# RWKV prepared two chunks at a time, with U of both heads in one PSUM bank and the rate kept as raw tanh

## The chip, the cores and the metric

The kernel runs on one core of one Trainium2 chip, in one launch. The metric is the device time of an execution in microseconds: 4006.45 before, the median of three runs (4003.45 to 4014.16).

## The reference

Two layers of a diffusion transformer with three token mixers side by side, all in fp32. 1024 latent tokens and 256 context tokens of width 1024 are normalised and projected; a gated linear attention, a grouped-query attention and an RWKV-7 branch of width 512 each give an output; three sigmoid gates weigh them, and a last projection is added to the residual. Only the RWKV branch is touched here. Cut to what matters, for 8 heads of 64, once forward and once backward over the tokens:

```python
w = jnp.exp(-RWKV_DECAY_SCALE * jax.nn.sigmoid(w0 + jnp.tanh(wd) @ wup))
a = jax.nn.sigmoid(a0 + ad @ aup)                 # the rate
kd = k * (1.0 + (a - 1.0) * k_a)                  # the key with its factor
def step(s, inp):                                 # token by token
    sa = jnp.einsum('bhvk,bhk->bhv', s, kk_t)
    s = (s * w_t[:, :, None, :] - sa[..., None] * (kk_t * a_t)[:, :, None, :]
         + v_t[..., None] * k_t[:, :, None, :])
    return s, jnp.einsum('bhvk,bhk->bhv', s, r_t)
```

The two directions are added, normalised per head, given a bonus term sum(r * (kf + kb) * r_k) * v and multiplied by silu of a gate.

## The kernel before

The scan is done in chunks of 64 tokens. Ten steps of 128 tokens, that is of two chunks c = 0, 1, go through each layer, and a step treats the forward block (d = 0) and the mirrored backward block (d = 1) together. Five pieces of code make up a step, each a Python generator whose `yield w` marks a place where other work may come between:

- **elem** (L863): loads lt, kk, k, r; eight program matmuls ps_t<-lt,wup per direction (the trace counts each fp32 matmul as two) give decay and rate before their tanh; ScalarE's tanh (L897) and GpSimd's `tensor_scalar` (L898) make the sigmoid (of the rate the negative one), VectorE's scan (L900) sums the decays, ScalarE's exponentials make Pt and its inverse, products on VectorE and GpSimd give AR (L910, L912) and BK (L920, L924). GpSimd multiplies kk by the rate (L919), forms the factor of the key in four quarters (L922), and multiplies by r for the bonus (L929), which goes out to wscr.
- **gram** (L933), for one chunk: eight program matmuls ps_t<-AR,BK for each direction, copied to Ms (ScalarE, L955) and under a mask to G (VectorE, L956); BK transposed to BKT. Ms goes to DRAM (nscr), and its 16x16 diagonal blocks come back as Lm. Thirty VectorE instructions on 64 partitions (mt L974 and acc L977 in turn) invert these unit triangles. The inverse goes out to tscr and, transposed, to dscr, and comes back whole as DT and Dg.
- **merge** (L990): the matmuls ps_u<-DT,G, then ps_u<-Dg,ET and two of ps_u<-T,ET build the inverse T of the whole 64x64 block.
- **chain** (L1027): the state. ps_a<-UV,G and ps_a<-S,AR make X, ps_a<-X,T makes U, which two copies (L1061 VectorE, L1063 ScalarE) write into UV; ps_a<-UV,BKT gives the next state S, and ps_a<-AR,S and ps_a<-G,UV the output.
- **finish** (L1119): normalisation and bonus of a block whose second direction is done.

`spread` interleaves generators by windows given as shares of a stage; `rwkv` (L1151) is a stage per chunk: the chain of chunk q over the whole of it, merge of q + 1, gram of q + 2, and in every other stage elem of the next step. `weave` puts this beside `merge_gates`, dense matmuls in triples of 512 columns (ps_mm or ps_o<-h,wh twice and <-h,wl once) that need nothing of RWKV and here are called fill; a fill matmul may be placed no earlier than eight yields before its place in the code. A scheduler then fixes the order of each engine's instructions, so that what stands in a queue waits for what is ahead of it. All DMAs are issued by SyncE's queue in the trace (SP), in order too, the fill's weights (wr) among them.

PSUM is used by tag: two banks "mm", two "a", two "t", one "u" and one "o".

Of the kernel before, what the change touches and what calls it, by code (L numbers as in the profile page):

```python
# [29 lines left out]
def consts():  # L30
# [8 lines left out]
    c["gmask"] = np.concatenate([np.concatenate([above, incl], 1), np.concatenate([strict, incl], 1)], 0)  # L39
# [26 lines left out]
    c["ident16"] = np.tile(np.eye(16, dtype=np.float32).reshape(1, 256), (64, 1))  # L66
# [4 lines left out]
def hybrid_kernel(ctx: ExitStack, tc: tile.TileContext, I: dict, C: dict, out: bass.AP):  # L71
# [102 lines left out]
    NSCR = 3  # L174
    nscr, dscr, tscr = [[dt(f"{x}scr{i}", [64, 1040]) for i in range(NSCR)] for x in "ndt"]

# [3 lines left out]
    def full(z):  # L180
        return z.rearrange("(u i) x -> u (i x)", i=4)[:, 0:4096].rearrange("u (s t) -> s u t", t=64)
# [120 lines left out]
    zero = zp.tile([64, 1040], F32, name="zero")  # L302
# [30 lines left out]
    for l in range(DEPTH):  # L333
# [73 lines left out]
        vec.tensor_scalar(out=prm[:, 6, :], in0=prm[:, 5, :], scalar1=-1.0, scalar2=None, op0=ALU.mult)  # L407
        vec.tensor_scalar(out=prm[:, 7, :], in0=prm[:, 5, :], scalar1=-1.0, scalar2=1.0, op0=ALU.mult, op1=ALU.add)
# [418 lines left out]
        gmask, id16 = rload("gmask", [128, 128]), rload("ident16", [64, 256])  # L827
# [35 lines left out]
        def elem(step):  # L863

            live = need_ctx or step >= 2
            o = {"AR": [], "BK": [], "PC": rp.tile([128, 2, 8], F32, tag="PC", bufs=3, name=nm("PC"))}
            ld = {}
            lt = re_.tile([128, 2, 128], F32, tag="lt", bufs=1, name=nm("lt"))
            for d in range(2):
                c = slice(128 * blk_of(step, d), 128 * blk_of(step, d) + 128)  # L870
                for j in range(2):
                    dma(out=lt[64 * j:64 * j + 64, d], in_=lora[64 * d:64 * d + 64, j, c])
                for x in ("kk", "k", "r"):
                    if x == "r" and not live:
                        continue
                    ld[x, d] = re_.tile([128, 4, 128], F32, tag="ld_" + x, bufs=2, name=nm("ld_" + x))
                    dma(out=ld[x, d], in_=rscr[x][:, c].rearrange("(m p) n -> p m n", p=128))
            for d in range(2):
                t0 = 128 * blk_of(step, d)

                def tk(x):
                    v = ld[x, d]
                    if d:
                        v = v[:, :, ::-1]
                    return v.rearrange("p m (c i) -> p m c i", c=2)

                sc, av = tmp(), tmp()
                pz = [ps("t"), ps("t")]
                for p in range(4):
                    for j in range(2):  # L890
                        hr = slice(64 * j, 64 * j + 64)
                        x = lt[hr, d, :]
                        pe.matmul(pz[j][:, 128 * p:128 * p + 128], wup[d][hr, 128 * p:128 * p + 128], x[:, ::-1] if d else x, start=True, stop=True)
                yield 1.8
                for j, dst, bi, s in ((0, sc, 0, 0.5), (1, av, 2, -0.5)):
                    for p in range(4):
                        act(out=dst[:, p, :], in_=pz[j][:, 128 * p:128 * p + 128], func=AF.Tanh, scale=0.5, bias=prm[:, bi + d, p:p + 1])  # L897
                    pool.tensor_scalar(out=dst, in0=dst, scalar1=s, scalar2=s, op0=ALU.mult, op1=ALU.add)  # L898
# [12 lines left out]
                if live:
                    vec.tensor_tensor(out=AR[:, :, :, 1, :], in0=Pv[:, :, :, 1:65], in1=tk("r"), op=ALU.mult)  # L912
                else:
                    vec.memset(AR[:, :, :, 1, :], 0.0)
                BK = rq.tile([128, 4, 2, 2, 64], F32, tag="BK", bufs=2, name=nm("BK"))
                av4 = av.rearrange("p m (c i) -> p m c i", c=2)
                ka = tmp()
                ka4 = ka.rearrange("p m (c i) -> p m c i", c=2)
                pool.tensor_tensor(out=ka4, in0=tk("kk"), in1=av4, op=ALU.mult)  # L919
                vec.tensor_tensor(out=BK[:, :, :, 0, :], in0=ka4, in1=Pi, op=ALU.mult)  # L920
                for p in range(4):
                    pool.tensor_scalar(out=av[:, p, :], in0=av[:, p, :], scalar1=prm[:, 6, p:p + 1], scalar2=prm[:, 7, p:p + 1], op0=ALU.mult, op1=ALU.add)  # L922
# [8 lines left out]
            return o

        def gram(q, es, step):  # L933

            c, e = q % 2, es[step]
            o = dict(e)
            G = rq.tile([128, 2, 2, 4, 128], F32, tag="G", bufs=3, name=nm("G"))
            BKT = rq.tile([128, 2, 4, 128], F32, tag="BKT", bufs=3, name=nm("BKT"))
            UV = rq.tile([128, 2, 4, 2, 64], F32, tag="UV", bufs=3, name=nm("UV"))
            Ms = rq.tile([64, 2, 2, 4, 64], F32, tag="Ms", bufs=1, name=nm("Ms"))  # L940
            o["G"], o["BKT"], o["UV"] = G, BKT, UV
            for d in range(2):
                t0 = 128 * blk_of(step, d)
                v = vtm[d, t0 + 64 * c:t0 + 64 * c + 64, :]
                dma(out=UV[64:128, d].rearrange("p m h i -> p (m h i)"), in_=v)
            for d in range(2):
                AR, BK = e["AR"][d], e["BK"][d]
                pg = [ps("t"), ps("t")]
                for p in range(4):
                    for h in range(2):  # L950
                        r = slice(64 * h, 64 * h + 64)
                        pe.matmul(pg[h][:, 128 * p:128 * p + 128], BK[r, p, c].rearrange("p a i -> p (a i)"), AR[r, p, c].rearrange("p a i -> p (a i)"), start=True, stop=True)
                yield 2.0
                for h in range(2):
                    act(out=Ms[:, h, d], in_=pg[h][0:64].rearrange("p (u i) -> p u i", u=4)[:, :, 0:64], func=AF.Copy)  # L955
                    vec.tensor_tensor(  # L956
                        out=G[:, h, d], in0=pg[h].rearrange("p (u i) -> p u i", u=4),
                        in1=gmask.unsqueeze(1).to_broadcast([128, 4, 128]), op=ALU.mult)
            ns, ds, ts = nscr[q % NSCR], dscr[q % NSCR], tscr[q % NSCR]
            dma(out=full(ns), in_=Ms.rearrange("p h d m t -> p (h d m) t"))  # L960
            Lm = rq.tile([64, 16, 16], F32, tag="Lm", bufs=1, name=nm("Lm"))
            dma(out=Lm, in_=diag(ns))
# [3 lines left out]
            for d in range(2):  # L966
                pt = ps("t")
                for p in range(4):
                    pe.transpose(pt[:, 128 * p:128 * p + 128], e["BK"][d][:, p, c].rearrange("p a i -> p (a i)"), ident)
# [401 lines left out]
```

## Time and profile before

| | |
|---|---|
| median of three runs | 4006.45 us (4003.45 to 4014.16) |
| the profiled execution | 3994.97 us, span 3993.2 us, mean granted clock 0.958 |
| TensorE busy | 3737.1 us, 94% |
| VectorE / ScalarE / GpSimd busy | 53% / 41% / 23% |
| the chain that ended last | TensorE 68%, DMA 11%, VectorE 8%, GpSimd 4% |
| DMA | 497 MB, mean 125 GB/s |

RWKV's first stretch lies at about 1040 to 1828 us (layer 0), the second at 3014 to 3752 us (layer 1). "Busy" is the time in which an instruction of the engine is under way; a matmul at the lower clock is busy for longer, so a high share is not yet full speed. Releasers in brackets say whose event ended a wait; where one instruction waited for several, the one that came last. A wait of an engine other than TensorE costs nothing as long as nobody on TensorE is reached by it.

### The profile page before, as it was taken

What the parts mean: (1) busy time and instruction counts of PE and PEld (TensorE: products, weight loads), DVE (VectorE), ACT (ScalarE), POOL (GpSimd) and SP (SyncE); (2) the same over time, 40 slices, a digit from 0 to 9 for tenths busy, and PEclk for the clock granted to TensorE, in tenths of its full rate; (3) what the DMA queues carried; (4) which work ended last, traced back from release to release, by engine and by line L of the source; (5) the groups of instructions that cost most, each with busy time, mean ns of one, the idle gap of its engine ahead of it and who ended that gap; (6) DMA issues with size and microseconds to landing.
All of it is one profiled execution on the core that took longest, in us unless ns stands there. A gap on an engine that the chain in (4) does not pass through costs nothing.

```text
span 3993.2 us, 82346 instructions
## 1 busy us (share of the span) xinstructions
PE 3737.1 (94%) x32356; PEld 3135.2 (79%) x32356; DVE 2101.7 (53%) x4932; ACT 1649.8 (41%) x4135; POOL 934.1 (23%) x1072
## 2 busy tenths in 40 slices
PE   5999999999889898899998999999998898988999
PEld 3699888888777787677877898888886776766787
DVE  3234445456576676654453244455565766665462
ACT  3244435456434444434133344354474334344322
POOL 2133220000232322310333042300002323223042
PEclk7999999999989999999999999999998899889999
DMA  7723225312365667556544132253124556655553
GB/s 228 247 59 89 55 79 169 103 54 84 99 146 124 143 157 187 146 135 193 159 139 132 52 96 70 76 159 116 48 70 108 117 128 143 152 136 134 178 157 113
DMA packets 826613, 497.24 MB, mean 125 GB/s; under 512 B 303152, under 2 KB 760176, under 8 KB 824176
## 3 DMA queue, kind: packets, MB, share of 16 engines
q1 hardware_dynamic: 826224, 491.97, 45.0%
q8 instruction: 254, 4.16, 0.5%
q14 instruction: 135, 1.11, 0.1%
HBM read 340.02 MB, written 151.81 MB: 123 GB/s over the span
## 4 chain that ended last, share of the span: by engine, by line
PE 68%; DMA 11%; DVE 8%; POOL 4%; issue 4%; ACT 3%; SPq 2%; POOLq 0%; DVEq 0%; ACTq 0%
PE ps_mm L85 27%; PE ps_a L85 17%; PE ps_o L85 12%; PE ps_u L85 6%; PE ps_t L90 3%; PE ps_t L85 2%; DMA nscr<-Ms 2%; DMA Lm<-nscr 2%; POOL tmp L922 1%; DVE mt L974 1%; DVE acc L977 1%; DMA wr<-in_w_in_dram 1%; DVE wl L343 1%; DMA tscr<-acc 1%; POOL tmp L919 1%
## 5 line engine op out<-in xcount | busy, mean ns | idle before, releaser
L85 PE MATMUL ps_mm<-h,wh 128*128 128x512 f32 (+1 forms) x2496 | 764.5, 389 | 10.1 <-ACT wh L342 7.7
L85 PEld LDWEIGHTS ps_mm<-h,wh 128*128 128x128 f32 x2496 | 452.5, 196 | 105.2 <-issue 11.7
L343 DVE TENSOR_TENSOR wl<-wr,wh 128x512 fp32r<-128x512 f32 (+1 forms) x464 | 334.5, 743 | 296.7 <-ACT wh L342 292.5
L85 PE MATMUL ps_mm<-h,wl 128*128 128x512 f32 (+1 forms) x1248 | 473.8, 380 | 1.7 <-DVE wl L343 1.7
L342 ACT ACTIVATE wh<-wr 128x512 fp32r<-128x512 f32 (+1 forms) x464 | 271.5, 622 | 420.1 <-PE ps_mm L85 161.4
L85 PE MATMUL ps_mm<-wh,h 128*128 128x256 f32 x2032 | 400.4, 290 | 9.5 <-ACT wh L342 5.9
L85 PEld LDWEIGHTS ps_mm<-wh,h 128*128 128x128 f32 x2032 | 327.7, 194 | 26.0 <-issue 10.7
L85 PE MATMUL ps_a<-h,wh 128*128 128x512 f32 (+1 forms) x1024 | 300.1, 369 | 0.0
L85 PE MATMUL ps_mm<-wl,h 128*128 128x256 f32 x1016 | 293.4, 289 | 0.4 <-DVE wl L343 0.2
L85 PE MATMUL ps_o<-h,wh 128*128 128x512 f32 (+1 forms) x928 | 287.7, 392 | 0.6 <-DVE M L1265 0.6
L85 PEld LDWEIGHTS ps_mm<-h,wl 128*128 128x128 f32 x1248 | 243.6, 195 | 47.8 <-issue 4.0
L974 DVE TENSOR_TENSOR mt<-Lm,acc 64x15 f32<-64x15 f32 (+2 forms) x600 | 129.4, 216 | 163.7 <-DMA Lm<-nscr 146.0
L803 POOL TENSOR_TENSOR y<-y,sg 128x128 f32<-128x128 f32 x64 | 30.2, 472 | 755.1 <-DVE nb L794 369.0
L85 PEld LDWEIGHTS ps_a<-h,wh 128*128 128x128 f32 x1024 | 183.7, 189 | 28.3
L85 PEld LDWEIGHTS ps_mm<-wl,h 128*128 128x128 f32 x1016 | 196.7, 194 | 7.4 <-issue 4.9
L85 PE MATMUL ps_o<-wh,h 128*128 128x256 f32 x976 | 196.7, 289 | 3.5 <-ACT h L286 3.2
L85 PEld LDWEIGHTS ps_o<-h,wh 128*128 128x128 f32 x928 | 167.9, 197 | 34.2 <-issue 2.2
L85 PE MATMUL ps_a<-h,wl 128*128 128x512 f32 (+1 forms) x512 | 188.6, 368 | 0.0
L776 DVE TENSOR_REDUCE mx<-ps_mm 128x1 f32<-128x512 f32 (+1 forms) x200 | 117.9, 594 | 111.1 <-PE ps_mm L85 108.0
L85 PE MATMUL ps_o<-h,wl 128*128 128x512 f32 (+1 forms) x464 | 176.1, 380 | 0.0
L85 PEld LDWEIGHTS ps_o<-wh,h 128*128 128x128 f32 x976 | 158.5, 193 | 10.7 <-issue 5.3
L1006 POOL COPY T<-Dg 128x512 f32<-128x512 f32 x40 | 30.0, 749 | 566.2 <-DMA Dg<-dscr 527.2
(326 smaller groups left out, 8125.2 us busy)
## 6 DMA issues: line engine op xcount, KB each, us to landing
wr<-in_w_in_dram SPq DMA_DIRECT2D x376, 256.0 KB, 3.5
tg<-th SPq DMA_DIRECT2D x96, 256.0 KB, 3.4
th<-tg SPq DMA_DIRECT2D x96, 256.0 KB, 2.9
wm<-in_w_mod_dram SPq DMA_DIRECT2D x16, 1024.0 KB, 7.1
ld_k<-rscr_k SPq DMA_DIRECT2D x40, 256.0 KB, 3.6
ld_kk<-rscr_kk SPq DMA_DIRECT2D x40, 256.0 KB, 3.7
UV<-vtm SPq DMA_DIRECT2D x80, 128.0 KB, 3.2
nscr<-Ms SPq DMA_DIRECT2D x40, 256.0 KB, 3.8
```

What stands on the lines that cost most here:

```text
L85: PE.last = nc.tensor.matmul(*a, **k)
L90: PE.last = nc.tensor.transpose(*a, **k)
L342: act(out=hi, in_=src, func=AF.Copy)
L343: vec.tensor_tensor(out=lo, in0=src, in1=hi.bitcast(F32), op=ALU.subtract)
L776: vec.tensor_reduce(out=mx[:, i:i + 1], in_=s[:, :n], axis=AX.X, op=ALU.max, negate=True)
L803: pool.tensor_tensor(out=y[:, hc], in0=y[:, hc], in1=sg[:, hc], op=ALU.mult)
L919: pool.tensor_tensor(out=ka4, in0=tk("kk"), in1=av4, op=ALU.mult)
L922: pool.tensor_scalar(out=av[:, p, :], in0=av[:, p, :], scalar1=prm[:, 6, p:p + 1], scalar2=prm[:, 7, p:p + 1], op0=ALU.mult, op1=ALU.add)
L974: vec.tensor_tensor(out=mt[:, :n, :w], in0=Lm[:, j, j + 1:16].unsqueeze(2).to_broadcast([64, n, w]), in1=acc[:, j:j + 1, :w].to_broadcast( ...
L977: vec.tensor_tensor(out=acc[:, j + 1:16, :w], in0=acc[:, j + 1:16, :w], in1=mt[:, :n, :w], op=ALU.add)
L1006: pool.tensor_copy(out=T.rearrange("p d m t -> p (d m t)"), in_=Dg.rearrange("p d m t -> p (d m t)"))
```

## The change

- `prep` takes the place of the windows for elem and gram: elem and gram of both chunks for d = 0, then for d = 1, then one `inverse` for both chunks on 128 partitions. Scratch tensors have 128 rows and there are two of each instead of three; DT takes a buffer of Ms (two in all), Dg has two, G and BKT have four; the UV load moves into merge.
- `rwkv` is a stage per step: both chains over the whole of it, merge of its second chunk in 0 to 0.35, prep of the next step in 0 to 0.6, merge of the next step's first chunk in 0.75 to 1.0.
- U of both heads goes into the two partition halves of one bank instead of two banks.
- The rate stays raw tanh: the scaling of it is left out, a VectorE instruction computes (tanh + 1) * kk where GpSimd multiplied, and the missing factor -0.5 stands in the mask of G, in the copies of Ms and (by `half`) of BKT. The factor of the key is made by four ScalarE copies with scale and bias instead of four GpSimd instructions.

The matmuls are the same in number and shape.

```diff
@@ key factor, rate
-                for j, dst, bi, s in ((0, sc, 0, 0.5), (1, av, 2, -0.5)):
...
-                    pool.tensor_scalar(out=dst, in0=dst, scalar1=s, scalar2=s, op0=ALU.mult, op1=ALU.add)
+            pool.tensor_scalar(out=sc, in0=sc, scalar1=0.5, scalar2=0.5, op0=ALU.mult, op1=ALU.add)
...
-                pool.tensor_tensor(out=ka4, in0=tk("kk"), in1=av4, op=ALU.mult)
+            vec.scalar_tensor_tensor(out=ka4, in0=av4, scalar=1.0, in1=tk("kk"), op0=ALU.add, op1=ALU.mult)
...
-                    pool.tensor_scalar(out=av[:, p, :], in0=av[:, p, :], scalar1=prm[:, 6, p:p + 1], scalar2=prm[:, 7, p:p + 1], op0=ALU.mult, op1=ALU.add)
+                act(out=BK[:, p, :, 1, :], in_=av4[:, p], func=AF.Identity, scale=prm[:, 6, p:p + 1], bias=prm[:, 7, p:p + 1])
@@ preparation
+        def prep(os, step):
+            e = {}
+            yield from elem(step, 0, e)
+            o = [chunk(step, c, e) for c in range(2)]
+            Ms = [None, None]
+            for c in range(2):
+                Ms[c] = rq.tile([64, 2, 2, 4, 64], F32, tag="Ms", bufs=2, name=nm("Ms"))
+                yield from gram(o[c], c, 0, Ms[c])
+            yield from elem(step, 1, e)
+            for c in range(2):
+                yield from gram(o[c], c, 1, Ms[c])
+                dma(out=full(nscr[step % NSCR], c), in_=Ms[c].rearrange("p h d m t -> p (h d m) t"))
+            yield from inverse(step, o)
+            os[2 * step], os[2 * step + 1] = o
...
-            Lm = rq.tile([64, 16, 16], F32, tag="Lm", bufs=1, name=nm("Lm"))
+            Lm = rq.tile([128, 16, 16], F32, tag="Lm", bufs=1, name=nm("Lm"))
...
+                if j % 5 == 4:
+                    yield 0.0
...
+            for c in range(2):
+                DT = o[c]["DT"] = rq.tile([64, 2, 2, 4, 64], F32, tag="Ms", bufs=2, name=nm("DT"))
+                dma(out=DT.rearrange("p h d m t -> p (h d m) t"), in_=full(ts, c))
@@ chain
-            pu = [ps("a"), ps("a")]
+            pu = ps("a")
...
-                        pe.matmul(pu[h][0:64, (4 * d + p) * 64:(4 * d + p) * 64 + 64], T[r, d, p, :], X[r, d, p, :], start=True, stop=True)
-            yield 1.8
+                        pe.matmul(pu[r, (4 * d + p) * 64:(4 * d + p) * 64 + 64], T[r, d, p, :], X[r, d, p, :], start=True, stop=True)
+            yield 1.3
@@ rwkv
-            for q in range(nq):
-                ths = [(chain(q, os.pop(q)), 0.0, 1.0, 8.3 + 6 * 2.0 + 12 * 2.0 if q % 2 else 8.3 + 6 * 2.0)]
-                if q + 1 < nq:
-                    ths.append((merge(os, q + 1), *((0.4, 0.9), (0.65, 1.0))[q % 2], 3.3 + 4 * 2.0))
-                if q + 2 < nq:
-                    ths.append((put(os, q + 2, gram(q + 2, es, (q + 2) // 2)), *((0.55, 0.9), (0.1, 0.5))[q % 2], 5.0 + 6 * 2.0))
...
+            for w in spread([(prep(os, 0), 0.0, 0.7, whole_prep), (merge(os, 0), 0.8, 1.0, whole_merge)]):
+                yield 2.5 * w
+            for step in range(NTILE):
+                ths = [(both(step), 0.0, 1.0, whole_chain), (merge(os, 2 * step + 1), 0.0, 0.35, whole_merge)]
+                if step + 1 < NTILE:
+                    ths.append((prep(os, step + 1), 0.0, 0.6, whole_prep))
+                    ths.append((merge(os, 2 * step + 2), 0.75, 1.0, whole_merge))
```

The order of the instructions moves at three places, shown here in layer 1. On TensorE before, these rows lead up to a first merge matmul (ps_u<-DT,G); the last gram of that chunk, which read BK_35540 with the chunk's other half, stands 79 rows further up (ps_t_35681).

```order
L90 MATMUL ps_t_36004<-c_ident,BK_35472 128x128 x4
L85 MATMUL ps_a_36012<-AR_34651,S_35715 64x64 x8
L85 MATMUL ps_a_36012<-AR_34719,S_35715 64x64 x8
L85 MATMUL ps_mm_36039<-h_23341,wh_36029 128x512 x2
L85 MATMUL ps_mm_36039<-h_23341,wl_36030 128x512
L90 MATMUL ps_t_36044<-c_ident,BK_35540 128x128 x4
L85 MATMUL ps_a_36012<-G_35087,UV_35089 64x64 x16
L85 MATMUL ps_mm_36039<-h_23342,wh_36029 128x512 x2
L85 MATMUL ps_mm_36039<-h_23342,wl_36030 128x512
L85 MATMUL ps_u_36114<-DT_35819,G_35657 64x48 x16
```

Between that gram and this merge stand a whole chunk's worth of other work: state, output, fill and the grams of the next chunk; by the durations of the trace 22.6 us. On TensorE after, at the place that corresponds to it, these rows follow each other; the last gram of the step (ps_t_33823, of AR_33753) stands 31 rows above the merge matmul, and between the two stand 7 matmuls ps_a<-UV,G, one set of four transposes, 16 matmuls ps_a<-S,AR, five fill triples, and the elem and gram matmuls of the next step whose end and beginning are shown.

```order
L85 MATMUL ps_t_34060<-lt_34049,wup_31850 128x128
L85 MATMUL ps_t_34061<-lt_34049,wup_31850 128x128
L85 MATMUL ps_a_34074<-S_33817,AR_33753 64x64 x7
L85 MATMUL ps_mm_33857<-h_22926,wh_33847 128x512 x2
L85 MATMUL ps_mm_33857<-h_22926,wl_33848 128x512
L85 MATMUL ps_t_34133<-AR_34113,BK_34116 128x128
L85 MATMUL ps_t_34134<-AR_34113,BK_34116 128x128
...
L85 MATMUL ps_t_34133<-AR_34113,BK_34116 128x128
L85 MATMUL ps_t_34134<-AR_34113,BK_34116 128x128
L85 MATMUL ps_u_33917<-DT_33902,G_33452 64x48 x16
```

The merge matmul has moved close behind the grams of its own step, and the first gram of the next step (AR_34113) stands ahead of it, close behind its elem. On VectorE the same step after reads as follows in the middle of its inverse (mt_33867, acc_33865); AR_34113 and BK_34116 are those of the gram above.

```order
L988 TENSOR_TENSOR mt_33867<-Lm_33863,acc_33865 128x10x6
L991 TENSOR_TENSOR acc_33865<-acc_33865,mt_33867 128x10x6
L988 TENSOR_TENSOR mt_33867<-Lm_33863,acc_33865 128x9x7
L950 TENSOR_TENSOR tmp_34059<-BK_34116,ld_k_34054 128x512
L991 TENSOR_TENSOR acc_33865<-acc_33865,mt_33867 128x9x7
L932 COPY PC_34048<-Pt_34108 128x8
L936 TENSOR_TENSOR AR_34113<-Pt_34108,ld_kk_34052 128x8x64
L938 TENSOR_TENSOR AR_34113<-Pt_34108,ld_r_34056 128x8x64
L988 TENSOR_TENSOR mt_33867<-Lm_33863,acc_33865 128x8x8
L949 TENSOR_TENSOR BK_34116<-tmp_34117,tmp_34106 128x8x64
L951 TENSOR_TENSOR BK_34116<-tmp_34059,tmp_34106 128x8x64
```

In before the same elem work stands behind the end of an inverse (here of acc_36815; L900, which the order prints as SCALAR_TENSOR_TENSOR, is the scan):

```order
L974 TENSOR_TENSOR mt_36815<-Lm_36811,acc_36813 64x15
L977 TENSOR_TENSOR acc_36813<-acc_36813,mt_36815 64x15
L900 SCALAR_TENSOR_TENSOR tmp_37084<-smask_32266,tmp_37056 128x512
L964 COPY acc_37407<-ident_32270 64x256
L1023 COPY T_36919<-ps_u_36976 32x8x32
L906 COPY PC_37038<-Pt_37086 128x8
L910 TENSOR_TENSOR AR_37091<-Pt_37086,ld_kk_37042 128x8x64
L912 TENSOR_TENSOR AR_37091<-Pt_37086,ld_r_37046 128x8x64
L920 TENSOR_TENSOR BK_37094<-tmp_37095,tmp_37084 128x8x64
```

The elem instructions have moved from behind an inverse into the middle of one. In SP's queue, the same step after has these issues from the loads of the next elem to the return of the inverse.

```order
L904 DMA ld_k_34827<-rscr_k 128x4x128
L904 DMA ld_kk_34825<-rscr_kk 128x4x128
L957 DMA wscr_108<-tmp_34117 128x4x128
L904 DMA ld_r_34829<-rscr_r 128x4x128
L994 DMA tscr_114<-acc_33865 128x16x16
L997 DMA dscr_112<-accT_33899 128x16x16
L1000 DMA DT_33902<-tscr_114 64x16x64
L1000 DMA DT_33907<-tscr_114 64x16x64
L1003 DMA Dg_33904<-dscr_112 64x8x64 x2
L1003 DMA Dg_33909<-dscr_112 64x8x64 x2
L1208 DMA wr_34973<-in_w_in_dram 128x4x128
```

What was issued for each chunk apart is issued for both chunks in one run, behind the loads of the next elem and ahead of a weight load of the fill.

## Rows read from the trace of the kernel before

**Rows 1.** Part 1 of the page: engine, busy us (share of the span), instructions.
```profile
PE 3737.1 (94%) x32356; PEld 3135.2 (79%) x32356; DVE 2101.7 (53%) x4932; ACT 1649.8 (41%) x4135; POOL 934.1 (23%) x1072
```

**Rows 2.** Two RWKV stretches: length, busy us (instructions) by engine, PEclk, DMA share, GB/s.
```profile
1040.00:1828.00 788.00, 702.33 (x9127) 575.62 (x9126) 507.41 (x1230) 325.25 (x738) 222.13 (x236) 0.93 0.61 148
3014.00:3752.00 738.00, 657.82 (x8432) 520.05 (x8430) 467.32 (x1171) 286.10 (x658) 210.25 (x220) 0.91 0.55 131
```

**Rows 3.** PE waits by releaser, layer 0 (1040 to 1800): total us, times, longest us.
```profile
PE ps_u L85 <- DVE T L1021: 13.9, 6, 4.0
PE ps_u L85 <- DMA DT<-tscr: 12.2, 6, 3.6
PE ps_t L85 <- DVE BK L924: 11.9, 3, 8.0
...
PE ps_a L85 <- ACT UV L1063: 7.2, 3, 4.0
```

**Rows 4.** The same, layer 1 (3005 to 3760).
```profile
PE ps_u L85 <- DMA DT<-tscr: 10.1, 5, 4.3
PE ps_u L85 <- DVE T L1023: 9.4, 6, 3.8
PE ps_t L85 <- ACT Pt L904: 9.0, 1, 9.0
PE ps_t L85 <- DVE BK L924: 8.7, 4, 5.6
```

**Rows 5.** One chunk by timelines of PE, SP, VectorE: start, length, work, [wait before].
```profile
1338.07 1.16 PE L85 MATMUL ps_t<-AR,BK 64*128 64x128 f32 x8
...
1339.66 0.62 SPq L960 DMA_DIRECT2D nscr<-Ms  x1
1343.38 0.60 SPq L962 DMA_DIRECT2D Lm<-nscr  x1
...
1346.05 0.18 DVE L974 TENSOR_TENSOR mt<-Lm,acc 64x15 f32<-64x15 f32 x1 [5.24 <-DMA Lm<-nscr]
...
1356.38 0.62 SPq L978 DMA_DIRECT2D tscr<-acc  x1
...
1358.93 0.59 SPq L983 DMA_DIRECT2D DT<-tscr  x1
```

**Rows 6.** DMA issues, layer 1: count, KB each, median us to landing.
```profile
nscr<-Ms SPq DMA_DIRECT2D x20, 256.0 KB, 4.2
DT<-tscr SPq DMA_DIRECT2D x20, 256.0 KB, 4.4
...
Lm<-nscr SPq DMA_DIRECT2D x20, 64.0 KB, 2.9
```

**Rows 7.** Part 5 of the page, the whole run: busy, mean ns, idle before, releasers.
```profile
L974 DVE TENSOR_TENSOR mt<-Lm,acc 64x15 f32<-64x15 f32 (+2 forms) x600 | 129.4, 216 | 163.7 <-DMA Lm<-nscr 146.0
```

**Rows 8.** PE timeline, a dense place of layer 1.
```profile
3229.15 0.63 PE L85 MATMUL ps_o<-h,wh 128*128 128x512 f32 x2
...
3229.94 1.15 PE L85 MATMUL ps_a<-UV,BKT 128*64 128x64 f32 x32
3231.02 0.73 PE L85 MATMUL ps_o<-h,wh 128*128 128x512 f32 x2
```

**Rows 9.** Groups by line, layer 1, columns as in rows 7.
```profile
L922 POOL TENSOR_SCALAR tmp<-tmp,prm 128x128 f32<-128x128 f32 x80 | 68.7, 869 | 1.7
...
L1061 DVE COPY UV<-ps_a 64x512 f32<-64x512 f32 x20 | 13.5, 677 | 3.2 <-PE ps_a L85 3.1
L1050 DVE TENSOR_TENSOR X<-ps_a,X 128x512 f32<-128x512 f32 x19 | 13.1, 690 | 1.9 <-PE ps_a L85 1.4
```

**Rows 10.** PE timeline, an elem group and the gram that follows it.
```profile
1051.28 1.71 PE L85 MATMUL ps_t<-lt,wup 64*128 64x128 f32 x16
...
1061.84 2.08 PE L85 MATMUL ps_t<-AR,BK 64*128 64x128 f32 x16 [7.96 <-DVE BK L924]
```

**Rows 11.** Windows behind that wait, columns as in rows 2.
```profile
1061.84:1067.40 5.56, 5.56 (x24) 4.59 (x25) 4.75 (x7) 1.79 (x4) 5.45 (x5) 0.50 0.76 209
```

More of the change, by code (lines that the diff above doesn't have):

```diff
@@ L172, in hybrid_kernel, with full @@
     yscr, wscr = dt("yscr", [512, NT]), [dt(f"wscr{i}", [512, NT]) for i in range(2)]
-    NSCR = 3
-    nscr, dscr, tscr = [[dt(f"{x}scr{i}", [64, 1040]) for i in range(NSCR)] for x in "ndt"]
+    NSCR = 2
+    nscr, dscr, tscr = [[dt(f"{x}scr{i}", [128, 1040]) for i in range(NSCR)] for x in "ndt"]
     def diag(z):
         return z[:, 0:1024].rearrange("p (s t) -> p s t", t=64)[:, :, 0:16]
-    def full(z):
-        return z.rearrange("(u i) x -> u (i x)", i=4)[:, 0:4096].rearrange("u (s t) -> s u t", t=64)
+    def full(z, c):
+        return z[64 * c:64 * c + 64].rearrange("(u i) x -> u (i x)", i=4)[:, 0:4096].rearrange("u (s t) -> s u t", t=64)
     def xrow(l, t):
@@ L301, in hybrid_kernel @@
     zpool, zp = popen(name=nm("zp"))
[L302 removed]
+    zero = zp.tile([128, 1040], F32, name="zero")
     vec.memset(zero, 0.0)
@@ L865, in elem, with chunk @@
+        def chunk(step, c, e):
+            o = {"AR": e["AR"], "BK": e["BK"], "PC": e["PC"]}
+            for x in ("G", "BKT"):
+                o[x] = rq.tile([128, 2, 2, 4, 128] if x == "G" else [128, 2, 4, 128], F32, tag=x, bufs=4, name=nm(x))
+            return o
+        def elem(step, d, o):
             live = need_ctx or step >= 2
-            o = {"AR": [], "BK": [], "PC": rp.tile([128, 2, 8], F32, tag="PC", bufs=3, name=nm("PC"))}
+            if d == 0:
+                o["AR"], o["BK"] = [], []
+                o["PC"] = rp.tile([128, 2, 8], F32, tag="PC", bufs=3, name=nm("PC"))
@@ L931, in elem @@
[L931 to L953, printed above, removed]
-                for h in range(2):
[L955 to L960, printed above, removed]
-            Lm = rq.tile([64, 16, 16], F32, tag="Lm", bufs=1, name=nm("Lm"))
@@ new lines, in elem @@
+            lt = re_.tile([128, 128], F32, tag="lt", bufs=2, name=nm("lt"))
+            c = slice(128 * blk_of(step, d), 128 * blk_of(step, d) + 128)
+            for j in range(2):
+                dma(out=lt[64 * j:64 * j + 64], in_=lora[64 * d:64 * d + 64, j, c])
+            for x in ("kk", "k", "r"):
+                if x == "r" and not live:
+                    continue
+                ld[x, d] = re_.tile([128, 4, 128], F32, tag="ld_" + x, bufs=2, name=nm("ld_" + x))
+                dma(out=ld[x, d], in_=rscr[x][:, c].rearrange("(m p) n -> p m n", p=128))
@@ new lines, in elem, with tk @@
+            t0 = 128 * blk_of(step, d)
+            def tk(x):
+                v = ld[x, d]
+                if d:
+                    v = v[:, :, ::-1]
+                return v.rearrange("p m (c i) -> p m c i", c=2)
+            sc, av = tmp(), tmp()
+            pz = [ps("t"), ps("t")]
+            for p in range(4):
+                for j in range(2):
+                    hr = slice(64 * j, 64 * j + 64)
+                    x = lt[hr, :]
+                    pe.matmul(pz[j][:, 128 * p:128 * p + 128], wup[d][hr, 128 * p:128 * p + 128], x[:, ::-1] if d else x, start=True, stop=True)
@@ L962, in gram, with inverse @@
+        def inverse(step, o):
+            ns, ds, ts = nscr[step % NSCR], dscr[step % NSCR], tscr[step % NSCR]
+            Lm = rq.tile([128, 16, 16], F32, tag="Lm", bufs=1, name=nm("Lm"))
             dma(out=Lm, in_=diag(ns))
-            acc = rq.tile([64, 16, 16], F32, tag="acc", bufs=1, name=nm("acc"))
+            acc = rq.tile([128, 16, 16], F32, tag="acc", bufs=1, name=nm("acc"))
             vec.tensor_copy(out=acc.rearrange("p a b -> p (a b)"), in_=id16)
-            mt = rq.tile([64, 16, 16], F32, tag="mt", bufs=1, name=nm("mt"))
@@ L966, in gram @@
[L966 to L969, printed above, removed]
-                yield 0.5
-                act(out=BKT[:, d].rearrange("p m i -> p (m i)"), in_=pt, func=AF.Copy)
+            mt = rq.tile([128, 16, 16], F32, tag="mt", bufs=1, name=nm("mt"))
             for j in range(15):
```

159 lines of the change are left out of this document (74 added, 85 removed).

## The prediction

> **What bounds the kernel now.** The page's first part comes first: TensorE is busy 94% of the span [rows 1], so the end moves only with what keeps TensorE idle or slow. The change edits the RWKV part of each layer alone, so I next read the windows of the two RWKV stretches [rows 2]: 788 us with 702.3 busy, and 738 us with 657.8 busy. That is 85.7 + 80.2 = 165.9 us idle, the most that could be won there by better order. The granted clock there is 0.93 and 0.91, that is, part of the time at the lower of the two levels (1.2 instead of 2.4 GHz): 788 x 0.07 x 2 = 110 us and 738 x 0.09 x 2 = 133 us at half speed, which cost half of that, 121 us. Third, the waits of TensorE [rows 3, 4]: no releaser dominates. DT, the transposed inverse coming back from DRAM, takes 12.2 + 10.1 us; T and UV, results that VectorE or ScalarE hand over, 13.9 + 7.2 + 9.4 of those shown; BK and Pt, keys and decays that the gram matmuls need, 11.9 + 8.7 + 9.0, of which 8.0 and 9.0 are one wait in each layer's prologue. Last, one chunk followed through three timelines [rows 5]: its last gram ends at 1338.07 + 1.16 = 1339.23, Ms leaves at 1339.66, Lm is asked for at 1343.38, the inverse starts on VectorE at 1346.05, its result leaves at 1356.38, DT is asked for at 1358.93, and DT takes 4.4 us to land [rows 6]: 19.7 + 4.4 = 24.1 us from the last gram to the first merge matmul (ps_u<-DT,G, called m0 below). TensorE hardly feels these 24 us because the order gives it some 26 us of other matmuls in between (the order rows of before: 22.6 us in the place shown). This cover is what the change alters.
>
> **The change part by part.**
>
> *Two chunks per preparation.* The transfers out and back and the 30-instruction inverse now occur once per step, 10 times a layer instead of 20. VectorE waits 146.0 us for Lm in the whole run [rows 7]; half of it may go. But VectorE is not the bound, and the order shows the other side. m0 of the first chunk now waits for the last gram of both chunks, and the prepared step is to be merged from 0.75 of the step on while its preparation is spread up to 0.6. I counted TensorE's work between the last gram of both chunks and that m0 in the order, with 0.79 us for three matmuls of 512 columns after other work and 1.08 for a group of sixteen 64-wide ones [rows 8]. Layer 1, step by step: 6.7, 7.8, 8.3, 13.4, 13.4, 13.4, 12.1, 20.0, 19.2, 21.1, sum 135; layer 0: 8.2, 10.6, 23.0, 16.0, 14.0, 17.8, 16.5, 27.6, 22.2, 21.8, sum 178. Against before's 26 that is half.
>
> The latency to be covered: 24.1 from the rows; plus 2.1, since with the instructions that the order places inside the inverse it holds VectorE 12.4 us on average instead of the 10.3 of [rows 5] (the pieces: 30 x 0.216 [rows 7] and on average some eight others of about 0.7 [rows 9]); plus 0.8, since the queue of SP has wscr, two or three ld tiles and a second DT ahead, 0.6 each to issue [rows 5], partly while the inverse still runs. That makes 27.0 per step. Lm and tscr on 128 instead of 64 rows are not in the trace: between nothing (the count of bytes doubles, the issue does not) and once more the 2.9 us of Lm [rows 6]; I take nothing, as the 256 KB nscr takes only 4.2 against 2.9 for the 64 KB Lm, and keep 2 x 2.9 per step for the range. The 128-partition mt and acc lie between the price of the 64-partition ones, 216 ns [rows 7], and twice that, 6.5 us more per step; I take the first, since of two VectorE instructions of 512 columns the one on 64 partitions takes 677 ns and the one on 128 takes 690 [rows 9].
>
> So 20 steps x 27.0 - (135 + 178) = 227 us of stall. The same count over before's 40 chunks gives 35 us where the trace has 22.3 at DT in 6 + 5 waits [rows 3, 4]: about one us too much in each, or a factor of 0.64. The first correction makes 207, the second 145; I take 200, near the first, because a stall as long as these leaves little slack to be found elsewhere. Part of it will appear at the gram rather than at m0: in the order of after, gram d0 of the next step stands one group of three matmuls behind its elem matmuls, where [rows 10] show 8.8 us from the end of elem to its gram when nothing blocks VectorE; and scan, AR and BK of that elem now stand inside the inverse, behind the wait for Lm. Both are one latency, and are counted once.
>
> The trace shows DMAs of 64 KB taking 2.9 us and of 256 KB 4.2 to 4.4 [rows 6], so bytes weigh little here. The Trainium skill (DMA: Bandwidth & Descriptors, Anatomy of one DMA) gives, for transfers issued by another engine than here, about 2.0 us fixed plus bytes over 436 GB/s; by that an extra 64 KB on Lm and tscr costs an estimated 0.15 us each, 6 us in all, which would make the sum 6 us more, and half the round trips would look like a clear win. The rows price the same change by its cover instead, and it is the cover that I follow.
>
> *What goes.* DT's waits of before, 22.3, are replaced by the new ones. T and UV wait partly because VectorE stands before Lm in its queue: 30.5 us shown, half of them, 15. Gram waits outside the prologue, 29.6 - 17.0, fall into the new stall: 13. Of the other 165.9 - 22.3 - 30.5 - 29.6 = 83.5 us, short waits scattered over the steps, I let a third, 28, fall into stretches where TensorE stands anyway. Sum 22 + 15 + 13 + 28 = 78.
>
> *The clock.* After a wait of 7.96 us the granted clock is 0.50 for the next 5.56 us [rows 10, 11]. I expect some 30 stalls of this kind, 167 us at half speed, and about 35 us elsewhere: 202 against 243, so the loss falls from 121 to 101: -20. The Trainium skill (TensorE: Matmul & The Clock Gate, HAM oscillation — how this bites in real kernels) says that a loop whose every turn waits long for a DMA pays the return to full clock in every turn; by it two long stalls in each of the 20 steps would put 40 x 5.56 = 222 us at half speed beside those 35, a loss of 129 and a sum 28 us above mine. The trace shows the single event, not how often it will come.
>
> *Rate and key factor.* In a layer twenty scalings and eighty quarter ones of 869 ns leave GpSimd (68.7 us for the eighty [rows 9]); eighty copies with a factor go to ScalarE and twenty products to VectorE, at the 690 ns of a product of that size [rows 9]. At most this takes four times 0.869 less 0.69 off an elem chain, 2.8 us; but that chain now stands behind Lm on VectorE. Net 0; the bounds are -28, those 2.8 us in ten steps, and +14, twenty products on the path. *U in one bank*: the same matmuls and the same copies, one more "a" bank free. Waits on UV are 7.2 in layer 0 [rows 3]; bounds -15 to 0, I take 0, because the wait is on data. The moved UV load is issued a step earlier than it is read: 0, hidden by the merge, bounds 0 to +10.
>
> Sum against the profiled run of 3994.97 us: +200 - 78 - 20 = +102, 4097; the median of the runs is 11.5 us above the profiled one, so 4108.
>
> **The rivals.** *A, faster.* TensorE reaches m0 late in any case and the inverse runs bare: latency 24.1 - (10.3 - 6.5) = 20.3, stalls by the same count about 107 - 20 = 87; and the DT, T, UV and gram waits go wholly (82) with half of the other 83.5, clock -40: 3995 + 87 - 124 - 40 = 3918, median 3930. For it: VectorE's waits for Lm halve, GpSimd is relieved. Against: in layer 1 seven of ten covers are under 14 us. Chance 0.16.
> *B, no change.* The latency of A with the removals of my forecast: +87 - 78 - 20 = -11, median 3996. Chance 0.09.
> *C, slower still.* SP's queue becomes the bound: wscr waits for a GpSimd product behind the next elem, and tscr, DT, Dg and then the weight loads of the fill stand behind it in order. If in each step this holds DT and the weights by two landings of 4 us [rows 6], 20 x 8 = 160: 4268. It decides where wscr is issued later than the inverse ends. Against: in the order AR and BK are done halfway through the inverse, so the product is asked for before tscr. Chance 0.08.
> The forecast itself, 0.67.
>
> **How the numbers follow.** The forecast's own range goes from the factor 0.64 (145 instead of 200: 4053) to both transfers dearer by 2.9 in every step (2 x 2.9 x 20 = 116 more: 4224), and 4040 to 4190 holds most of it. The 80% range is 3950 to 4195, which leaves out part of A and nearly all of C. A measurement of this kernel tells about 0.3%, 12 us, from no change. Slower: 0.67 + 0.08, less 0.01 for the forecast's lower edge: 0.74; same 0.09 + 0.01 = 0.10; faster 0.16.
>
> **What would show it.** Right: TensorE's waits list DT<-tscr first with 10 to 20 entries and 70 to 130 us, the gram behind BK or the scan next with about as much, idle time of the two stretches 270 to 300 us, the stretches of layer 0 and 1 longer by about 30 and 70 us (covers of 178 and 135 against the same latency); VectorE's wait for Lm near half. Wrong: DT waits under 40 us (cover longer or latency under 20), or idle time as before with a higher clock; a wait of tscr or wr loads in SP's queue as the longest would be C.

## The result and the profile after

4116.52 us after (4108.11 to 4123.01) against 4007.47 before on the same chip: 1.0269 times as long [1.0245, 1.0293]. Forecast 4108. The profiled execution spans 4106.3 us. Here are part 1 of its page and then the windows of the two RWKV stretches (columns as in [rows 2]):

```profile
PE 3733.9 (91%) x32356; PEld 3146.7 (77%) x32356; DVE 1984.7 (48%) x4356; ACT 1706.0 (42%) x4275; POOL 695.2 (17%) x832
```
```profile
1036.00:1872.00 836.00, 701.10 (x9095) 579.51 (x9094) 446.81 (x941) 350.33 (x805) 109.30 (x116) 0.89 0.59 138
3057.00:3856.00 799.00, 643.15 (x8390) 515.36 (x8389) 408.57 (x883) 313.16 (x725) 85.23 (x100) 0.88 0.52 120
```

The stretches are 48 and 61 us longer, all of it idle time of TensorE: 134.9 + 155.9 = 290.8 us against 165.9 [rows 2]. TensorE's waits by releaser, in the stretch of layer 0 and then in that of layer 1 (as [rows 3, 4]):

```profile
PE ps_u L85 <- DMA DT<-tscr: 48.0, 7, 9.5
PE ps_t L85 <- DVE Pt L928: 46.1, 7, 9.4
PE ps_a L85 <- ACT tmp L1153: 14.8, 4, 5.7
PE ps_u L85 <- DVE T L1040: 5.4, 3, 4.4
PE ps_t L85 <- DVE BK L951: 4.5, 3, 2.8
```
```profile
PE ps_u L85 <- DMA DT<-tscr: 65.4, 8, 10.9
PE ps_t L85 <- DVE Pt L928: 52.1, 7, 9.4
PE ps_a L85 <- ACT tmp L1153: 13.4, 3, 5.1
PE ps_t L85 <- DVE mt L988: 7.8, 1, 7.8
PE ps_t L85 <- DVE BK L951: 7.4, 3, 4.2
```

DT takes 113.4 us in 15 waits, and the gram 46.1 + 4.5 + 52.1 + 7.8 + 7.4 = 117.9. (Pt L928 is a memset of 0.07 us that ends beside the last BK product, and mt an instruction next to it; the gram waits for BK.) The wait at tmp of finish (L1153), 6.1 us at the same line of before, has grown to 28.2, which I had not forecast; the wait behind the rsqrt that finish calls (tmp L158) fell from 11.8 to 2.5. VectorE's wait for Lm fell from 146.0 [rows 7] to

```profile
DVE mt L988 <- DMA Lm<-nscr: 84.1, 20, 6.7
```

One step of layer 1 by the timelines of TensorE, SP, and GpSimd with VectorE, as [rows 5]:

```profile
3166.72 1.16 PE L85 MATMUL ps_t<-AR,BK 64*128 64x128 f32 x8
...
3172.35 1.71 PE L85 MATMUL ps_t<-lt,wup 64*128 64x128 f32 x16
...
3182.79 2.08 PE L85 MATMUL ps_t<-AR,BK 64*128 64x128 f32 x16 [7.46 <-DVE Pt L928]
3195.77 1.95 PE L85 MATMUL ps_u<-DT,G 64*64 64x48 f32 x32 [10.90 <-DMA DT<-tscr]
```
```profile
3172.78 0.36 SPq L982 DMA_DIRECT2D Lm<-nscr  x1
...
3188.54 0.36 SPq L994 DMA_DIRECT2D tscr<-acc  x1
3189.20 0.65 SPq L997 DMA_DIRECT2D dscr<-accT  x1
3191.59 1.32 SPq L1000 DMA_DIRECT2D DT<-tscr  x2
```
```profile
3174.83 0.62 POOL L924 TENSOR_SCALAR tmp<-tmp 128x512 f32<-128x512 f32 x1 [23.24 <-issue]
...
3175.56 0.18 DVE L988 TENSOR_TENSOR mt<-Lm,acc 128x15 f32<-128x15 f32 x1 [6.55 <-DMA Lm<-nscr]
...
3177.04 1.22 DVE L926 TENSOR_TENSOR_SCAN tmp<-smask,tmp 128x512 f32<-128x512 f32 x1
...
3181.96 0.69 DVE L951 TENSOR_TENSOR BK<-tmp,tmp 128x512 f32<-128x512 f32 x1
...
3188.34 0.17 DVE L991 TENSOR_TENSOR acc<-acc,mt 128x15 f32<-128x15 f32 x1
```

The last gram of both chunks ends at 3167.88. TensorE then has 7.5 us of other work, reaches the next step's gram and stands 7.46 us. That gram comes 8.73 us after its elem matmuls (3172.35 + 1.71), as long as the 8.8 of [rows 10], so most of this wait is the elem chain itself; the inverse adds little, since scan could start behind GpSimd's scaling at 3175.45 and starts at 3177.04. TensorE does the gram in 2.08 us, has nothing more ahead of m0 and stands 10.90 us for DT. That makes 3195.77 - 3167.88 = 27.9 us of latency, 9.5 of them covered. And the clock over the same step (columns as in [rows 2]):

```profile
3168.00:3175.20 7.20, 7.20 (x65) 5.46 (x64) 0.69 (x1) 2.63 (x9) 0.37 (x1) 1.00 0.44 57
3182.79:3184.87 2.08, 2.08 (x16) 1.78 (x16) 1.94 (x5) 0.00 (x0) 0.98 (x1) 0.50 0.27 77
3184.87:3195.77 10.90, 0.00 (x0) 0.00 (x0) 3.42 (x17) 0.63 (x1) 0.00 (x0) 0.50 0.65 117
3195.77:3203.40 7.63, 7.63 (x73) 6.02 (x74) 4.01 (x6) 2.71 (x7) 1.46 (x2) 0.50 0.80 138
3179.59:3203.48 23.89, 9.79 (x90) 7.91 (x91) 12.58 (x36) 3.34 (x8) 3.05 (x3) 0.50 0.64 123
```

After each of the two waits TensorE works at 0.50, the 1.2 GHz level: 2.08 + 7.63 = 9.7 us in this step. The third line matters for the reading: the 10.90 us in which TensorE does nothing are entered at 0.50 too. The last line is the whole spell at 0.50: 23.89 us, of which TensorE is busy for 9.79.

### The profile page after: what moved, and what is told of

It is laid out like the page before. It is cut to its first block, busy times and chain, and to the rows that moved or that the text cites. A ratio compares the mean times of both kernels' runs of the same rounds, so it can differ in the third digit from the quotient of the medians.

```text
span 4106.3 us, 81420 instructions
## 1 busy us (share of the span) xinstructions
PE 3733.9 (91%) x32356; PEld 3146.7 (77%) x32356; DVE 1984.7 (48%) x4356; ACT 1706.0 (42%) x4275; POOL 695.2 (17%) x832
## 5 line engine op out<-in xcount | busy, mean ns | idle before, releaser
L85 PE MATMUL ps_mm<-h,wh 128*128 128x512 f32 (+1 forms) x2496 | 754.4, 384 | 9.0 <-ACT h L342 5.7
L85 PE MATMUL ps_t<-AR,BK 64*128 64x128 f32 x1280 | 154.6, 319 | 118.3 <-DVE Pt L928 98.2
L85 PEld LDWEIGHTS ps_t<-AR,BK 64*128 64x128 f32 x1280 | 130.2, 218 | 145.6 <-issue 128.1
L970 DVE TENSOR_TENSOR G<-ps_t,gmask 128x512 f32<-128x512 f32 x160 | 105.1, 687 | 220.0 <-ACT Ms L969 219.5
L85 PEld LDWEIGHTS ps_a<-h,wh 128*128 128x128 f32 x1024 | 183.7, 189 | 28.2
L776 DVE TENSOR_REDUCE mx<-ps_mm 128x1 f32<-128x512 f32 (+1 forms) x200 | 117.9, 593 | 110.9 <-PE ps_mm L85 107.9
L85 PE MATMUL ps_u<-DT,G 64*64 64x48 f32 x1280 | 61.2, 259 | 114.3 <-DMA DT<-tscr 113.4
```

The costliest lines, as they stand in the source:

```text
L85: PE.last = nc.tensor.matmul(*a, **k)
L776: vec.tensor_reduce(out=mx[:, i:i + 1], in_=s[:, :n], axis=AX.X, op=ALU.max, negate=True)
L970: vec.tensor_tensor(out=o["G"][:, h, d], in0=pg[h].rearrange("p (u i) -> p u i", u=4), in1=gmask.unsqueeze(1).to_broadcast([128, 4, 128]), ...
```

## The experiments

**One: the parts apart.** The scalings, the key factor and U can be had without the two-chunk structure, and the structure without them. `small` is before with the rate, key factor and U hunks; `rate_only` and `u_only` split it; `struct` is the change with those hunks reversed.

```diff
 # small: before, and of the change only
...
+            vec.scalar_tensor_tensor(out=ka4, in0=av4, scalar=1.0, in1=tk("kk"), op0=ALU.add, op1=ALU.mult)
...
+                act(out=BK[:, p, :, 1, :], in_=av4[:, p], func=AF.Identity, scale=prm[:, 6, p:p + 1], bias=prm[:, 7, p:p + 1])
...
+            pu = ps("a")
...
 # struct: the changed kernel, but
-            pool.tensor_scalar(out=sc, in0=sc, scalar1=0.5, scalar2=0.5, op0=ALU.mult, op1=ALU.add)
...
+                pool.tensor_scalar(out=dst, in0=dst, scalar1=s, scalar2=s, op0=ALU.mult, op1=ALU.add)
...
-            pu = ps("a")
+            pu = [ps("a"), ps("a")]
```

> The kernel before with the small edits alone: U of both heads in one bank, raw tanh rate, key factor on ScalarE; one chunk per preparation as before. Theory (cover: only the distance between gram and first merge matters): the covers in the order are those of before, about 26 us, so 4007 us plus or minus 12, with GpSimd's busy time in the RWKV stretches less than half. Rival (the small edits carry part of the loss, by more work on VectorE and ScalarE): 4025 to 4060.

> The kernel before with raw tanh rate and key factor on ScalarE as its only edits. Theory (the rate edit gives the gain): 0.988 to 0.993, VectorE's elem products nearer to 690 ns than to 760 to 920, and GpSimd under 120 us in the first stretch. Rival (the bank gives it): 0.997 to 1.003.

> The kernel before with U of both heads in one bank as its only edit. The small edits together gave a ratio of 0.9898 to before. Theory (the rate edit gives it, by taking GpSimd out of the elem chain and out of VectorE's way): 0.997 to 1.003. Rival (the freed bank of tag a lets the state's matmuls start earlier): 0.990 to 0.995, with the waits on UV, X and T smaller than before.

> The changed kernel with the rate, the key factor and U's two banks as before, so that only the preparation of two chunks at a time and its windows remain. Theory (the parts add): the changed kernel stands at 1.0269 and the small edits at 0.9898, so 1.034 to 1.041, with DT waits of 110 us or more. Rival (the small edits gain nothing where the elem chain is hidden by the wait for the inverse): 1.024 to 1.030.

`small` 0.9898 [0.9883, 0.9914], 3954.3 against 3995.29: 41 us faster, where I had put nothing. `rate_only` 0.9915 [0.9897, 0.9932]; `u_only` 0.9988 [0.9978, 0.9998], in its bounds of -15 to 0. `struct` 1.0384 [1.0367, 1.0401], 4151.34 against 3993.15. `rate_only`, `u_only` and `struct` came out as expected; `small` didn't. So the bundle hid a gain and a larger loss, and within the intervals they multiply: 1.0384 x 0.9898 = 1.0278, the change 1.0269. Where the gain of `small` lies, its windows:

```profile
1039.00:1797.00 758.00, 690.08 (x9101) 560.56 (x9101) 499.61 (x1250) 354.66 (x815) 111.94 (x116) 0.95 0.63 153
2990.00:3698.00 708.00, 639.45 (x8387) 506.05 (x8388) 463.67 (x1192) 318.54 (x735) 94.19 (x100) 0.92 0.57 136
```

TensorE's idle time is 136.5 us against 165.9, and GpSimd's busy time is half of that in [rows 2]. The wait of ScalarE's exponentials for the scan, in before and in `small`, and beside it the four copies per elem pass that `small` gives to ScalarE:

```profile
ACT Pt L904 <- DVE tmp L900: 104.4, 36, 7.0
```
```profile
ACT Pt L908 <- DVE tmp L904: 37.5, 22, 3.6
```
```profile
L925 ACT ACTIVATE BK<-tmp,prm 128x128 f32<-128x128 f32 x160 | 67.3, 502 | 0.0
```

And VectorE's product that finishes BK, layer 1, in before and in `small` (columns as in [rows 7]):

```profile
L924 DVE TENSOR_TENSOR BK<-tmp,tmp 128x512 f32<-128x512 f32 x20 | 18.4, 921 | 0.3
```
```profile
L928 DVE TENSOR_TENSOR BK<-tmp,tmp 128x512 f32<-128x512 f32 x20 | 15.1, 754 | 0.0
```

The wait is 66.9 us shorter, but the copies, which all stand ahead of the exponentials, take 67.3: ScalarE works where it stood before, and the exponentials come little earlier (on average 8.0 instead of 9.1 us after the elem matmuls, 8.7 in `rate_only`). The gain in the elem chain lies behind them: from the start of the first exponential to the end of BK it is 8.0 us in before and 5.3 in `small`, the mean over the 40 passes. That is 2.7 us, close to the price of the removed instructions, 2.8 in the prediction. The product's mean is 167 ns shorter; over the whole run its median stays at 0.69 us, so this comes from a few long ones. Does GpSimd's mere activity cost something? `noise` puts 160 GpSimd instructions back into `small`, on a tile that nobody reads:

```diff
+                for p in range(4):
+                    pool.tensor_scalar(out=idle, in0=idle, scalar1=0.5, scalar2=0.5, op0=ALU.mult, op1=ALU.add)
```

> The kernel before with the small edits, and four GpSimd tensor_scalar of 128x128 per direction and step on a buffer that nobody else reads, issued after the bonus product: the same count and size as the key factor's instructions that the edit removed, but off the elem chain. Theory (the rate edit gains by a shorter chain from elem to gram): 0.988 to 0.992, as the small edits alone (0.9898). Rival (it gains because VectorE is slowed whenever GpSimd works): 0.994 to 1.000, with VectorE's elem products slowed from about 690 to 760 or more.

0.9949 [0.9934, 0.9964], between the two: in the rival's range, but without its sign. The instructions take 63.2 us at 395 ns each (the removed quarter ones took 869 [rows 9]), VectorE's products don't slow (690 and 791 ns, against 701 and 782 in `small`), and the chain from exponential to BK stays at 5.5 us, yet half of the gain is gone. So this much activity doesn't stretch VectorE. Of the 28 us by which the profiled run is longer than that of `small`, 18 are busy time of TensorE, which works 247 us at the granted clock 0.50 instead of 208. Why it does so stays open.

**Two: the round trip.** `zero_dt` reads DT and Dg from a scratch tensor of zeros that nothing in the step writes, so the merge gets no inverse; the inverse is still computed and sent out. The hunk of Dg is like the one shown.

```diff
-                dma(out=DT.rearrange("p h d m t -> p (h d m) t"), in_=full(ts, c))
+                dma(out=DT.rearrange("p h d m t -> p (h d m) t"), in_=full(zscr, c))
```

> The changed kernel, but DT and Dg are read from a scratch tensor of zeros that is written once at the start, so that the merge no longer waits for the inverse (the inverse is still computed and sent out; the output is not the reference's). Theory (latency from last gram to first merge): the 113 us of waits on DT go, and VectorE's inverse delays the next gram less; 3960 to 4010 us. Rival (the chain of state or the queue of SP has the same length and TensorE would wait elsewhere): the waits move to other releasers and the time stays above 4080.

0.9867 [0.9842, 0.9893], 3941.62 us, faster than the 3960 to 4010 expected. The waits for DT fall to 5.0 us, and the gram's fall with them to about a third (whole run):

```profile
PE ps_u L85 <- DVE T L1045: 26.9, 12, 5.0
PE ps_t L85 <- DVE BK L954: 21.9, 10, 5.8
PE ps_t L85 <- DVE Pt L931: 19.7, 4, 6.8
```

The inverse coming back is thus worth 4% in the changed kernel, more than DT's own 113 us of waits. With the trip for nothing the changed kernel, in this order and with this fill, stands at 0.9867, hardly below `small` at 0.9898, which has one trip per chunk.

**Three: the two stalls apart, and more cover.** `elem1st` puts both directions' elem ahead of all grams, so that no gram waits behind its own step's elem; `e1lead16` lets the fill be taken 16 yields early besides.

```diff
             yield from elem(step, 0, e)
+            yield from elem(step, 1, e)
...
-            yield from elem(step, 1, e)
...
-            weave(rwkv(), merge_gates(), (0.6, 0.53)[l], (0, 8), None)
+            weave(rwkv(), merge_gates(), (0.6, 0.53)[l], (0, 16), None)   # e1lead16
```

> The changed kernel with the order inside prep altered: elem of both directions first, then the grams of chunk 0, then those of chunk 1. In the order the covers between the last gram and the first merge grow from 313 to 380 us in sum over the 20 steps, and the distance from elem to the first gram from 1 to 6 us in most steps. Theory (cover): 67 us less of stall at the merge and some 10 to 30 less at the gram: 4020 to 4050 us, DT waits 60 to 80 us. Rival (latency of two-chunk transfers or the load on the engines decides, not the order): within 15 us of 4116.

> As elem1st, and fill matmuls may be hoisted by 16 yields instead of 8. Covers 468 us in sum, elem to gram about 9 us. Theory (cover): stalls at the merge 70 to 90 us by the count, less as measured; 3960 to 4010 us. Rival (hoisted fill only waits for its weights, so that the wait moves from DT to wh or wr): 4030 to 4120 with wh or wr among the first releasers.

`elem1st` 1.0125 [1.011, 1.014], `e1lead16` 0.9967 [0.9955, 0.9979], both in the range expected. In `elem1st` the gram's waits shrink from 118 to 43 us, but DT's, expected at 60 to 80, grow (whole run):

```profile
PE ps_u L85 <- DMA DT<-tscr: 134.9, 19, 15.8
PE ps_t L85 <- DVE BK L950: 20.0, 6, 6.3
PE ps_t L85 <- DVE Pt L927: 12.2, 2, 6.2
PE ps_t L85 <- ACT BK L947: 11.0, 2, 6.6
```

Two steps in which both elems run inside the inverse take 18.6 and 19.7 us from the first mt to the last acc, and 35 us to m0. The two stalls are one latency, as the prediction had it, but not a fixed one: what stands inside the inverse lengthens it. The covers, measured as TensorE's busy time between the last gram and m0 and summed over the 20 steps, are 337 us in the changed kernel, 396 in `elem1st` and 476 in `e1lead16` (380 and 468 were forecast for the two), and the time falls with each.

**Four: cover bought with fill.** In `smallhi`, `sm75` and `e1lead16hi` the weave's ratio is raised, so that more fill is placed in each RWKV step.

```diff
-            weave(rwkv(), merge_gates(), (0.6, 0.53)[l], (0, 8), None)
+            weave(rwkv(), merge_gates(), (0.65, 0.58)[l], (0, 8), None)   # smallhi: small with it
+            weave(rwkv(), merge_gates(), (0.75, 0.67)[l], (0, 8), None)   # sm75: small with it
+            weave(rwkv(), merge_gates(), (0.7, 0.62)[l], (0, 16), None)   # e1lead16hi: elem1st with it
```

> The kernel before with the small edits, and the fill woven in somewhat denser (0.65 and 0.58 of the weight of the RWKV work instead of 0.6 and 0.53). Covers before the first merges are longer in the order (sum over 40 chunks about 5% more). Theory (cover): 3 to 20 us faster than the small edits alone, 0.985 to 0.989 of before. Rival (the fill is used up earlier and the last steps stand bare): 0.990 to 0.996.

> The small edits on the kernel before, with the fill woven in at 0.75 and 0.67 (0.65 and 0.58 gave 0.9845). Covers grow by another 4% over 40 chunks. Theory (cover, with fill left to the end): 0.978 to 0.984. Rival (the fill runs out before the last steps): above 0.986, with the waits of the last 150 us of each stretch grown.

> Two chunks per preparation with elem of both directions first, fill hoisted by up to 16 yields and woven in at 0.7 and 0.62: covers 465 us over the 20 steps, about those of e1lead16 (468), but elem to gram 11 us instead of 9. Theory (cover, with the inverse lengthened by what stands inside it): 0.985 to 0.995. Rival (two chunks at a time are as good as one once covered): 0.975 to 0.985, at or below the small edits with the same weight of fill.

`smallhi` 0.9845 [0.9828, 0.9862], `sm75` 0.9807 [0.9793, 0.9822] at 3921.59 us, `e1lead16hi` 0.985 [0.9834, 0.9867] at 3936.08. The time of `e1lead16hi` lies where the two expected ranges meet and doesn't decide between them. One chunk at a time with more fill beats both kernels; two chunks at a time, with their order and cover (488 us) mended, reach `smallhi` but not `sm75`. The weights of fill differ, though: two chunks at a time with 0.75, or `small` with the lead of 16, was not run. The waits for DT over the whole run, `sm75` and then `e1lead16hi`:

```profile
PE ps_u L85 <- DMA DT<-tscr: 10.3, 6, 4.0
```
```profile
PE ps_u L85 <- DMA DT<-tscr: 73.5, 10, 15.1
```

## Why the prediction came out, and where it was wrong

**The cover: right.** Forecast: 27.0 us from the last gram to m0 and half of before's cover. The measured covers sum to 189 us in layer 0 and 148 in layer 1, for 178 and 135 forecast; each of the twenty lies 0.1 to 2.2 us above its count. Those of before were 22.6 to 43.0 us, 31.2 on average and not 26, which fits that the prediction's count gave it too much stall. The latency: the seven steps of layer 1 that stall by 8.3 to 10.9 us have 25.4, 27.9, 28.2, 29.7, 30.4, 29.1 and 30.8, mean 28.8; at the last three, with covers forecast at 19 to 21, m0 waits 0.2 or less. The 1.8 us missing, by parts: gram to mt 7.4 (6.8 taken), from there to tscr's issue 13.6 (12.4), to DT's issue 3.7 (2.55 + 0.8), DT to m0 4.1 (4.4). Stalls at DT and gram are 113.4 + 117.9 = 231.3, and before's at DT, BK and Pt 22.3 + 29.6 = 51.9, so +179, for a forecast of 200 - 22 - 13 = +165. Both stalls stand where the prediction put them, DT first with 15 entries and the gram with about as much. The split by layer was off: the stretches grew by 48 and 61 us, not by 30 and 70.

**What goes: right in sum.** The rest of the idle time fell from 165.9 - 51.9 = 114.0 to 290.8 - 231.3 = 59.5, by 55, with the 28.2 of finish inside; forecast 15 + 28 = 43.

**The clock: mis-sized, and not for the reason given.** I took 1 - PEclk of each stretch as time at half speed and forecast -20, from 243 us at half speed to 202. That recipe counts idle time entered at 0.50 as work; by it the change would stand at 836 x 0.11 x 2 + 799 x 0.12 x 2 = 376 us. If the trace's clock records are laid over TensorE's busy time, before's two stretches have 98.3 + 115.5 = 213.8 us of busy time at 0.50, and those after 99.7 + 92.3 = 192.0; another 35 and 180 us at 0.50 are idle. So the count for after was near, the value of before was 29 us too high, and the term is half of 22, -11. Over the whole run the busy time at 0.50 is 259 us before, 229 after, 208 in `small` and 265 in `struct`: half of the differences from before is -15, -26 and +3. Longer but fewer stalls, the reason given, gained nothing; what the clock gave back came with the small edits. One profile stands for each kernel, and the granted clock of the four runs after goes from 0.943 to 0.947, with the profiled one highest, so these sizes are loose.

The busy time of equal matmuls (x32356 in every run) is no better measure of the clock: it is 3737.1 us before, 3733.9 after, 3720.9 in `small` and

```profile
PE 3773.7 (91%) x32356; PEld 3175.6 (77%) x32356; DVE 2002.7 (48%) x4316; ACT 1643.5 (40%) x4115; POOL 916.6 (22%) x1072
```

in `struct`, 37 us above before, of which the lower level explains 3. The rest lies in matmuls at the full clock; why they take longer in this order is open. The Trainium skill (TensorE: Matmul & The Clock Gate, HAM oscillation — how this bites in real kernels) says that such a loop pays the slow clock in every turn. The trace agrees in so far as m0 starts at 0.50 in 17 of the 20 steps. The 222 + 35 = 257 us that the prediction worked out beside it did not come, 192 did: in the step shown both waits fall into one spell at 0.50, and before had its 214 us as well.

**Rate and key factor: the step failed.** "That chain now stands behind Lm ... Net 0, bounds -28 to +14". It gives 0.9915 alone, -30 us in the medians (3962.89 against 3993.15), just past the bound; and 1.0269 / 1.0384 = 0.989 together with U in the changed kernel. The price of 2.8 us was about right: from the first exponential to the end of BK an elem pass takes 7.0 us in `struct` and 4.8 in the changed kernel, so standing behind Lm doesn't hide it. What failed was to net it to 0, and to count it ten times in the bound where the kernel has 40 such passes. Part of the gain isn't idle time either: the profiled span of `rate_only` is 27 us shorter than before's, 15 of them busy time of TensorE, with 221 us at 0.50 instead of 259.

**How it adds up.** Span, idle and busy of TensorE in the profiled runs: the change +113 = +116 idle - 3 busy; `struct` +157 = +120 idle + 37 busy; `small` -46 = -30 idle - 16 busy. The forecast was +102 = +122 idle - 20 for the clock + 0 for the rest. The structure's idle time came as forecast. The other two terms, +37 and -46 for a forecast of -20 and 0, nearly cancel: that the total came within 9 us of 4108 is luck in part.

**Rivals.** A (TensorE late anyway, inverse bare) gave both stalls together 87 us, and they are 231. B fails with it. C would show in SP's queue: in the step above tscr leaves 0.03 us after the last acc, and DT 3.05 us behind it, which is tscr's landing. The transfers' size was cheap as taken, below. One cause beside the order was not tested: DT takes a buffer of Ms, two in all, and a gram takes both "t" banks until its copies are done. In the step above the gram that ends at 3184.87 is copied to Ms only after m0,

```profile
3198.21 0.64 ACT L969 ACTIVATE Ms<-ps_t 64x256 f32<-64x256 f32 x2
```

and TensorE can take no further gram until then. Whether buffers of DT's own would put more work ahead of m0, no run shows.

## What to carry to other kernels

Here halving the number of round trips through DRAM lost, because the work that stood in the waiting engine's queue between the last producer and the first consumer was cut with it, from 31 us to 17 per trip. Count that work in the order, per step, against the latency read from one followed chunk. Price a change of clock by the busy time that lies at the lower level, not by the mean granted clock of a stretch with idle time in it. When an engine's wait shrinks, look whether new work of its own fills it before you call the chain shorter. Of a bundled change, time the small edits apart, since a right sum can be made of two wrong terms.

## What the runs showed of the hardware

Twice the bytes cost little. The landing of four transfers of layer 1 after the change:

```profile
nscr<-Ms SPq DMA_DIRECT2D x20, 256.0 KB, 3.5
...
Lm<-nscr SPq DMA_DIRECT2D x10, 128.0 KB, 2.9
tscr<-acc SPq DMA_DIRECT2D x10, 128.0 KB, 3.3
dscr<-accT SPq DMA_DIRECT2D x10, 128.0 KB, 4.1
```

Lm takes 2.9 us with 64 KB [rows 6] and with 128 KB; tscr went from 2.5 to 3.3 and dscr from 3.4 to 4.1 (layer 1 of both traces). Transfers whose size stayed moved by as much, nscr from 4.2 to 3.5 and DT from 4.4 to 4.9, so the growth is no clear price of the bytes. The estimate of 0.15 us for 64 KB more that the prediction worked out from the Trainium skill (DMA: Bandwidth & Descriptors, Anatomy of one DMA) lies between 0 and 0.8. Of the inverse, mt and acc on 128 partitions take 0.17 to 0.23 us in the step above, but for one of 1.28, against a mean of 0.216 on 64 [rows 7]; over the whole run their mean is 0.230, so twice the partitions cost 6% more.
